# Moving the first FFN's and the branch stage's tiles by 192 bytes in SBUF

## The chip, the cores and the metric

The kernel runs on one core of one Trainium2 chip. The metric is the device time of one execution in microseconds (us). A matmul needs two instructions on TensorE (PE): a weight load, which puts the stationary operand (128 by 128 numbers) into the array, and the matmul itself, which streams the moving operand (here mostly 128 partitions by 512 fp32 numbers) through it into PSUM, the accumulator memory. Both operands lie in SBUF, the on-chip memory of 128 partitions; "the address" of a tile is its byte offset within a partition.

## The reference

One layer on 512 tokens of width 1024, in fp32:

```python
mod = silu(c) @ w_ada + b_ada                  # nine vectors: sh, sc, g for three parts
u = rms_norm(x) * (1 + sc1) + sh1
x = x + 0.5 * g1 * (silu(u @ Wa) * (u @ Wb)) @ ffn1_w_out     # FFN of inner width 2816
u = rms_norm(x) * (1 + sc2) + sh2
z = u @ w_mix + b_mix                          # q, k, v, gates of two branches
y_a = sigmoid(o) * norm(mlstm(q, k, v, i, f))  # 4 heads
y_b = forgetting_attention(q, k, v, f)         # 16 heads of 64
merged = sigmoid(g_a) * (y_a @ w_branch_a) + sigmoid(g_b) * (y_b @ w_branch_b)
x = x + g2 * (merged @ w_out)
u = rms_norm(x) * (1 + sc3) + sh3
x = x + 0.5 * g3 * (silu(u @ Wa2) * (u @ Wb2)) @ ffn2_w_out
```

## The kernel before

**Products in three parts.** Every large product is computed from operands that are split into a high and a low part: `split` (L92 to 105) copies a weight chunk to `wh` on ScalarE (ACT, L102) and subtracts to get `wl` on VectorE (DVE, L104). `mm3` then issues three matmuls, high by high (L127), high by low (L128) and low by high (L129); which operand is the stationary one depends on the stage:

```python
        pin(mm(ps, lh, rh, start=start, stop=False))      # L127: lh stationary, rh moving
        pin(mm(ps, lh, rl, start=False, stop=False))      # L128
        self.last_mm = pin(mm(ps, ll, rh, start=False, stop=stop))   # L129
```

In the profile a group is written out<-moving,stationary with the tiles' names, so `t<-wh,A` streams a weight tile `wh` against the stationary tile `A` and writes PSUM tile `t`.

**Stages and their operands, in order of time.**

- Start (to about 60 us) and the first FFN's input product `ffn_in` (to 268 us): weights `wh`, `wl` stationary, the normed input `uh`, `ul` moving.
- The first FFN's output product `pair_out` (268 to 379 us): stationary are the activations `A1`, `A2` (tags A0 to A10) and their rest tiles `Ra`, `Rb`; moving are the weights `wh`, `wl`. It runs over 11 pairs of row blocks twice: the first pass has 18 matmuls a pair, the second 24, so 462 in all. The second pass adds what the first left to `x` (`onto`, L600) and loads `x` again for that. For the last three pairs a part of the weights is prepared early in tiles `we`, which lie in the same pool as `A`; they are the moving operand of 36 of the matmuls.
- The norm between FFN and mixer, the gates and the attention stage (to about 845 us): two kinds of heads, whose small matmuls and transposes are mixed by hand with the large products of `w_mix`.
- The branch stage (845 to 970 us): `branch` makes 16 products of 24 matmuls, weights stationary, `yh`, `yl` moving; then `token_gemm` multiplies by `w_out` in two halves of 96 matmuls, here `mh`, `ml` stationary and weights moving.
- The second FFN (to the end), the same code as the first: `ffn_in_halves`, `ffn_in`, `pair_out`.

**Order.** Each engine takes its instructions in program order. Loads of weights are issued by SyncE (SP) in program order into a ring of three `raw` tiles; `wh` and `wl` are rings of four. So the chain that feeds PE is: load into `raw`, ACT makes `wh`, DVE makes `wl`; a tile of the rings comes free when PE has used it.

**Where the tiles lie.** Tiles are laid out in pools, one pool behind the other, each tile rounded up to 32 bytes. The pools `w` (weights), `u`, `x` and `y` hold for all or most of the kernel. Behind them pools are opened and closed: `f1t`, `st`, `f1h` for the first FFN, then `y`, and behind it `gates`, `att` (attention) and `br` (branch), then `f2t`, `f2h` for the second FFN. In the program as laid out before the change the tiles that matmuls read start at these addresses modulo 256:

| tiles | pool | address modulo 256 |
|---|---|---|
| weights `raw`, `wh`, `wl`; `uh`, `ul`; `x`; all of the `qk` ring | w, u, x, y | 160 |
| `A1`, `A2`, `Ra`, `Rb`, `we` of the first FFN | f1h, f1t | 224 (rest tiles of pairs 0 to 3: 160, in `x`) |
| `W`, `S`, `P` tiles, `tok` tiles of the attention | att | 0 |
| `vm` ring of the attention | att | 64, 128, 192 |
| `mh`, `ml`, `yh`, `yl`, `sg` of the branch stage | br | 224 |
| `A1`, `A2`, `Ra`, `Rb`, `we` of the second FFN | f2h | 160 |

The 224 comes from two small tiles. In `f1t`, `warm` (4 bytes) and `z22` (16 bytes) take 32 bytes each and stand ahead of everything else but two tiles of 512 bytes: 160 + 64 = 224. In `y`, `hgg` (64 bytes) is the last tile: 160 + 64 = 224 for the pools behind it. All large tiles are multiples of 256 bytes, apart from those of the ring `vm` and three of 32 bytes in `att`.

Of the kernel before, what the change touches and what calls it, by code (L numbers as in the profile page):

```python
# [11 lines left out]
F32 = mybir.dt.float32  # L12
F32R = mybir.dt.float32r
I32 = mybir.dt.int32
AF = mybir.ActivationFunctionType
# [5 lines left out]
P = 128  # L21
# [3 lines left out]
NK = 8  # L25
# [22 lines left out]
class Layer:  # L48
# [109 lines left out]
    def consts(self, tp):  # L158
        nc, cp, A = self.nc, self.cp, self.A
        row = lambda ap: ap.rearrange("o (r p) -> (o r) p", p=P)  # L160
        bm = A["b_mix"]

        self.rowsC = tp.tile([32, P], F32, name="rowsC")
        for r, ap in ((0, row(A["c"])), (8, row(A["ffn1_norm_g"])), (16, row(A["b_ada"][:, 0:2048]))):
            nc.scalar.dma_start(self.rowsC[r:r + ap.shape[0], :], ap)
        self.ident = cp.tile([P, P], F32, name="ident")
        make_identity(nc, self.ident)
        self.one = cp.tile([P, 1], F32, name="one")
        nc.gpsimd.memset(self.one, 1.0)
        self.rowsA = tp.tile([P, P], F32, name="rowsA")  # L170
        put = lambda r, ap: nc.gpsimd.dma_start(self.rowsA[r:r + ap.shape[0], :], ap)
        put(R_N2, row(A["mix_norm_g"]))
        put(R_N3, row(A["ffn2_norm_g"]))
        put(R_CW, A["conv_w"][0].rearrange("j (m p) -> (j m) p", p=P))
        put(R_CB, row(A["conv_b"]))
        put(R_QK, row(bm[:, 0:1024]))
        put(R_GG, row(bm[:, GA:GA + 2048]))
        put(R_MG, A["mlstm_norm_g"][0].rearrange("h (r p) -> (h r) p", p=P))
        put(R_FQ, A["fox_q_norm_g"][0].rearrange("(r h) p -> r (h p)", h=2))
        put(R_FK, A["fox_k_norm_g"][0].rearrange("(r h) p -> r (h p)", h=2))  # L180
        put(R_OM, row(bm[:, OM:OM + 1024]))

        warm = tp.tile([P, 1], F32, name="warm")
        nc.scalar.activation(warm, self.one, AF.Silu)
        z = tp.tile([P, 2, 2], F32, name="z22")
        nc.gpsimd.memset(z, 0.0)
        for h in range(2):
            nc.gpsimd.memset(z[:, h, h:h + 1], 1.0)

        self.unit = cp.tile([P, 2, 2], F32R, name="unit")  # L190
        nc.scalar.activation(self.unit, z, AF.Copy)
        self.mod_d = self.dp.tile([9, D], F32, name="mod_d")
# [1089 lines left out]
    def run(self):  # L1282
        nc, tc, A = self.nc, self.tc, self.A
# [133 lines left out]
        yp = ys.enter_context(tc.tile_pool(name="y", bufs=1))  # L1417
# [18 lines left out]
        with tc.tile_pool(name="att", bufs=1) as ip:  # L1436
            self.maskM = ip.tile([P, P], F32, name="maskM")
            self.maskF = ip.tile([P, P], F32, name="maskF")
            for t, fill, sgn in ((self.maskM, BIG, 1), (self.maskF, -BIG, -1)):

                nc.gpsimd.memset(t, 0.0)
                nc.gpsimd.affine_select(t, t, pattern=[[sgn, P]], compare_op=ALU.is_ge, fill=fill,
                                        base=0, channel_multiplier=-sgn)
            self.onz = ip.tile([P, NT, 2], F32, name="onz")
            nc.gpsimd.memset(self.onz[:, :, 0:1], 1.0)
            nc.gpsimd.memset(self.onz[:, :, 1:2], 0.0)
            self.hom = ip.tile([P, NK], F32, name="hom")
            nc.vector.tensor_scalar(self.hom, self.colA[:, R_OM:R_OM + NK], 0.5, None, op0=MUL)
            self.hmg = ip.tile([P, NK], F32, name="hmg")
            nc.vector.tensor_scalar(self.hmg, self.colA[:, R_MG:R_MG + NK], 0.5, None, op0=MUL)  # L1450
            self.hgg = yp.tile([P, 2 * NK], F32, name="hgg")
            nc.vector.tensor_scalar(self.hgg, self.colA[:, R_GG:R_GG + 2 * NK], 0.5, None, op0=MUL)
            self.klz = [None] * 2
            self.vt, self.W, self.fx, self.qkt, self.S = [None] * 4, {}, {}, {}, {}
            def advance(gen, n):
                for _ in range(n):
                    next(gen, None)
            advance(self.v_mlstm(0, ip, ip), 99)

            gates = iter([(m, i) for i in range(2) for m in range(NK)][2:])  # L1460
            def with_gates(gen, n):
                yield from gen
                for m, i in (next(gates) for _ in range(n)):
                    yield from self.gate(m, i, ip)
            for h0, n, fill in ((0, 3, with_gates(self.v_mlstm(1, ip, ip), 1)), (2, 4, with_gates(self.fox_qkv(0, ip), 3))):
                for f, h in ((self.mlstm_w, h0), (self.mlstm_w, h0 + 1), (self.mlstm_h, h0), (self.mlstm_h, h0 + 1)):
                    f(h, ip)
                    advance(fill, n)
                    if f == self.mlstm_h and h == 2:
                        self.fox_t(0, yp)  # L1470
                advance(fill, 99)
            for n in range(18):
                if n % 4 == 0 and n < 16:
                    advance(fill, 99)
                    g = n // 4
                    fill = with_gates(self.fox_qkv(g + 1, ip), (2, 2, 6)[g]) if g < 3 else (s for m in range(NK) for s in self.y_a(m, yp, ip))
                last = n >= 12
                if n < 16:
                    self.fox_s(n, ip)
                    advance(fill, 4 if n == 0 else 3 if n == 1 else 1 if last else 2)  # L1480
                if n >= 2:
                    self.fox_o(n - 2, ip)
                    advance(fill, 1)
                if n % 2 and n < 13:
                    self.fox_t((n + 1) // 2, yp)
                    if n == 11:
                        self.fox_t(7, yp)
                if 1 <= n < 17:
                    self.fox_p(n - 1, ip)
                    advance(fill, 1 if last else 2)  # L1490
            advance(fill, 99)
            for m in range(NK):
                self.dump(f"ya_{m}", self.ya[m])
                self.dump(f"yb_{m}", self.yb[m])
# [94 lines left out]
```

## Time and profile before

| | |
|---|---|
| median of 3 runs | 1327.01 us (1326.8 to 1328.08) |
| the profiled execution | 1328.68 us, span 1326.9 us from its first to its last instruction |
| PE busy | 1308.3 us, 99% of the span, 6332 matmuls |
| DVE, ACT, POOL busy | 959.9, 622.6, 43.8 us |
| PE's share of the chain that ended last | 91% |
| DMA | 254.18 MB, mean 192 GB/s |

A matmul of 512 columns is shown with a duration of about 0.39 us, though the next one starts after about 0.23 us: they overlap. So the busy time of PE says little, and what counts is the distance from start to start. The duration shown is that distance plus a constant, which is why a group whose matmuls follow one another more slowly by some ns shows a mean that is longer by the same ns.

### The profile page before, as it was taken

The page shows a single profiled execution, that of the slowest core. Times are in us where ns is not written, and L with a number is a line of the kernel's source. Part 1 is how long each engine was busy: PE and PEld are TensorE (multiplying, and loading weights), DVE is VectorE, ACT ScalarE, POOL GpSimd, SP SyncE. Part 2 cuts the span into 40 slices and gives each one's busy share as a digit, 9 for nine tenths or more (in the row PEclk, how much of TensorE's full clock was granted, in tenths as well). Part 3 has the DMA queues.
Part 4 walks back from the last instruction along what each step waited for, and adds up shares of the span by engine and source line. Part 5 has one row for each costly group of instructions (what it writes and reads, how often), then busy time and mean ns, then how long its engine had stood idle before and what let it go on. Part 6 is the DMA issues. An engine that isn't in the chain of part 4 may idle for free.

```text
span 1326.9 us, 17767 instructions
## 1 busy us (share of the span) xinstructions
PE 1308.3 (99%) x6332; PEld 1091.9 (82%) x6332; DVE 959.9 (72%) x1740; ACT 622.6 (47%) x1038; POOL 43.8 (3%) x65
## 2 busy tenths in 40 slices
PE   7999999999999999999999999999999999999998
PEld 6788888888789888888888788888788888888886
DVE  6877777467788687887887778677577656635777
ACT  5533232355476555566566666334263223223742
POOL 1000000000010101000000000003010000000000
PEclk9999999999999999999999999999999999999999
DMA  9899978464845334533342536687429768624574
GB/s 291 265 325 306 315 269 280 127 194 155 291 133 139 110 108 130 159 103 111 91 122 76 170 96 204 214 256 227 155 92 339 264 235 277 210 97 140 170 260 152
DMA packets 204345, 254.18 MB, mean 192 GB/s; under 512 B 14993, under 2 KB 146481, under 8 KB 204257
## 3 DMA queue, kind: packets, MB, share of 16 engines
q1 hardware_dynamic: 203872, 252.98, 59.9%
q8 instruction: 50, 0.82, 0.2%
q14 instruction: 39, 0.31, 0.1%
q0 software_dynamic: 320, 0.06, 0.0%
q10 hardware_dynamic: 64, 0.02, 0.0%
HBM read 217.28 MB, written 35.72 MB: 191 GB/s over the span
## 4 chain that ended last, share of the span: by engine, by line
PE 91%; DVE 4%; ACT 2%; DMA 2%; issue 1%; POOL 0%; SPq 0%; ACTq 0%; DVEq 0%; POOLq 0%
PE g L127 23%; PE g L129 23%; PE g L128 23%; PE t L128 4%; PE t L127 4%; PE t L129 4%; PE g L825 2%; PE t L1208 1%; PE t L1178 1%; DMA x<-x_d 1%; DVE wl L104 1%; PE t L1149 1%; PE t L825 1%; PE t L1150 1%; ACT wh L102 0%
## 5 line engine op out<-in xcount | busy, mean ns | idle before, releaser
L102 ACT ACTIVATE wh<-raw 128x1024 fp32r<-128x1024 f32 (+2 forms) x250 | 253.9, 1018 | 383.0 <-PE g L128 118.4
L104 DVE TENSOR_TENSOR wl<-raw,wh 128x1024 fp32r<-128x1024 f32 (+2 forms) x250 | 292.9, 1174 | 178.0 <-ACT wh L102 154.8
L128 PE MATMUL g<-ul,wh 128*128 128x512 f32 (+1 forms) x912 | 348.1, 383 | 1.0 <-POOL ul L267 1.0
L127 PE MATMUL g<-uh,wh 128*128 128x512 f32 (+1 forms) x912 | 348.5, 384 | 0.0
L129 PE MATMUL g<-uh,wl 128*128 128x512 f32 (+1 forms) x912 | 348.2, 382 | 0.0
L128 PEld LDWEIGHTS g<-ul,wh 128*128 128x128 f32 x912 | 171.3, 188 | 34.3 <-POOL ul L267 1.8
L129 PEld LDWEIGHTS g<-uh,wl 128*128 128x128 f32 x912 | 171.4, 188 | 33.2
L127 PEld LDWEIGHTS g<-uh,wh 128*128 128x128 f32 x912 | 171.0, 188 | 32.8 <-issue 0.6
L325 DVE SCALAR_TENSOR_TENSOR acc<-raw,ccol,acc 128x512 f32<-128x512 f32 (+1 forms) x70 | 66.8, 975 | 43.0 <-DMA raw<-in_w_ada_dram 42.6
L127 PE MATMUL g<-wh,uh 128*128 128x512 f32 (+1 forms) x256 | 97.4, 380 | 0.0
L129 PE MATMUL g<-wh,ul 128*128 128x512 f32 (+1 forms) x256 | 96.6, 377 | 0.0
L128 PE MATMUL g<-wl,uh 128*128 128x512 f32 (+1 forms) x256 | 96.4, 377 | 0.0
L128 PE MATMUL t<-wl,A 128*128 128x512 f32 x176 | 69.3, 394 | 1.7 <-DVE wl L104 1.6
L127 PE MATMUL t<-wh,A 128*128 128x512 f32 x176 | 69.3, 394 | 0.1
L129 PEld LDWEIGHTS g<-wh,ul 128*128 128x128 f32 x256 | 48.2, 188 | 9.0
L127 PEld LDWEIGHTS g<-wh,uh 128*128 128x128 f32 x256 | 48.2, 188 | 8.7 <-DVE tk L1046 0.5
L128 PEld LDWEIGHTS g<-wl,uh 128*128 128x128 f32 x256 | 48.2, 188 | 8.3
L127 PE MATMUL g<-yh,wh 128*128 128x512 f32 x128 | 50.4, 394 | 0.0
L129 PE MATMUL g<-yh,wl 128*128 128x512 f32 x128 | 50.2, 392 | 0.0
L128 PE MATMUL g<-yl,wh 128*128 128x512 f32 x128 | 49.7, 388 | 0.0
L455 ACT ACTIVATE A<-E 128x768 fp32r<-128x768 f32 x22 | 18.6, 846 | 56.5 <-DVE E L454 50.6
L1160 ACT ACTIVATE S<-S,mn 128x128 f32<-128x128 f32 (+1 forms) x64 | 35.5, 556 | 16.1 <-DVE mn L1152 9.9
(343 smaller groups left out, 2187.5 us busy)
## 6 DMA issues: line engine op xcount, KB each, us to landing
raw<-in_ffn_w_in_dram SPq DMA_DIRECT2D x82, 512.0 KB, 5.2
raw<-in_w_ada_dram SPq DMA_DIRECT2D x56, 512.0 KB, 5.1
raw<-in_w_mix_dram SPq DMA_DIRECT2D x46, 512.0 KB, 4.3
sa<-in_ffn_w_out_dram SPq DMA_DIRECT2D x22, 512.0 KB, 5.4
sb<-in_ffn_w_out_dram SPq DMA_DIRECT2D x44, 256.0 KB, 5.9
ws<-sa SPq DMA_DIRECT2D x22, 512.0 KB, 4.5
ws<-sb SPq DMA_DIRECT2D x44, 256.0 KB, 4.1
raw<-ws SPq DMA_DIRECT2D x44, 256.0 KB, 3.4
```

The source lines that it names most:

```text
L102: nc.scalar.activation(hi, src, AF.Copy)
L104: self.last_lo = nc.vector.tensor_tensor(lo, src, hi, op=SUB)
L127: pin(mm(ps, lh, rh, start=start, stop=False))
L128: pin(mm(ps, lh, rl, start=False, stop=False))
L129: self.last_mm = pin(mm(ps, ll, rh, start=False, stop=stop))
L325: nc.vector.scalar_tensor_tensor(a, r[:, s], c, a, op0=MUL, op1=ADD)
L455: nc.scalar.activation(A1[:, 0:3, :], E[:, 0:3, :], AF.Copy)
L825: pin(nc.tensor.matmul(acc_ps[b], (wl if p == 1 else wh)[:, b % 2, s], self.ul[k] if p == 2 else self.uh[k], start=k == 0 and p == 0, stop ...
L1149: nc.tensor.matmul(ps[:, :w], q[:, s], k[:, :w], start=True, stop=False)
L1150: nc.tensor.matmul(ps[:, :w], q[:, s], kl[:, :w], start=False, stop=True)
L1160: nc.scalar.activation(S[:, ws], S[:, ws], AF.Exp, scale=-1.0, bias=m, accum_out=sm[:, qb:qb + 1])
L1178: tr = lambda b, c, qb, kb: nc.tensor.transpose(b[:, c:c + P], S[:, P_OFF[qb] + kb * P:P_OFF[qb] + (kb + 1) * P], self.ident)
```

## The change

Two tiles get more bytes, and what is read and written of them stays the same: `warm` goes from 4 to 224 bytes, `hgg` from 64 to 256. All that lies behind them in SBUF moves up by 192 bytes: in the first FFN the rest of `f1t`, `st` and `f1h`; later `gates`, `att` and `br`. No instruction is added, removed or moved.

```diff
-        warm = tp.tile([P, 1], F32, name="warm")
-        nc.scalar.activation(warm, self.one, AF.Silu)
+        warm = tp.tile([P, 56], F32, name="warm")
+        nc.scalar.activation(warm[:, 0:1], self.one, AF.Silu)
...
-            self.hgg = yp.tile([P, 2 * NK], F32, name="hgg")
+            self.hgg = yp.tile([P, 64], F32, name="hgg")[:, 0:2 * NK]
```

After it, 224 in the table becomes 160 in `f1h`, `f1t` and `br`, 0 becomes 192 in `att`, and the `vm` ring goes to 0, 64, 128. The second FFN's pools do not move, since `f2t` starts where `f1t` and `y` start.

## The prediction

> **What bounds the kernel now.** I began with the page: who is busy, what the clock was, what the last chain consists of.
>
> ```profile
> span 1326.9 us, 17767 instructions
> PE 1308.3 (99%) x6332; PEld 1091.9 (82%) x6332; DVE 959.9 (72%) x1740; ACT 622.6 (47%) x1038; POOL 43.8 (3%) x65
> PEclk9999999999999999999999999999999999999999
> PE 91%; DVE 4%; ACT 2%; DMA 2%; issue 1%; POOL 0%; SPq 0%; ACTq 0%; DVEq 0%; POOLq 0%
> ```
>
> PE sets the end almost everywhere and the granted clock is at 90% or more in every slice, so a change of the time must come from the distance between matmuls or from the few places where PE waits. The change adds no work. The question is only whether that distance depends on where the operands lie. This trace can answer it, because the same code runs twice: the first FFN's output product with its stationary tiles at 224 modulo 256, the second's with them at 160, where the weights are. Next, then, the groups of matmuls with their mean durations, first for the first FFN (268 to 381 us):
>
> ```profile
> L127 PE MATMUL t<-wh,A 128*128 128x512 f32 x88 | 35.0, 398 | 0.1
> ...
> L129 PE MATMUL t<-wh,Ra 128*128 128x512 f32 x20 | 7.9, 396 | 0.0
> ...
> L129 PE MATMUL g<-we,Ra 128*128 128x512 f32 x6 | 2.3, 390 | 0.0
> L129 PE MATMUL g<-we,Rb 128*128 128x512 f32 x6 | 2.3, 389 | 0.0
> ```
>
> and the same view of the second FFN (1215 to 1324 us):
>
> ```profile
> L127 PE MATMUL t<-wh,A 128*128 128x512 f32 x88 | 34.3, 389 | 0.0
> ...
> L127 PE MATMUL g<-wh,A 128*128 128x512 f32 x54 | 20.7, 389 | 0.0
> ...
> L129 PE MATMUL t<-wh,Ra 128*128 128x512 f32 x20 | 7.8, 390 | 0.0
> ```
>
> The reader is to see 396 to 398 ns where moving and stationary operand differ by 64 modulo 256, and 389 to 390 where they agree. The two `we` groups are the control: they run in the first FFN, a few us after the others, with stationary tiles still at 224, but their moving tile lies in the same pool, at 224 too, and they take 389 to 390. So it is not the stage, and not the address itself; it is the difference between the two. The branch stage (845 to 969 us) has both roles reversed:
>
> ```profile
> L129 PE MATMUL g<-yh,wl 128*128 128x512 f32 x113 | 44.3, 392 | 0.0
> L127 PE MATMUL g<-yh,wh 128*128 128x512 f32 x112 | 44.1, 394 | 0.0
> L128 PE MATMUL g<-yl,wh 128*128 128x512 f32 x112 | 43.5, 388 | 0.0
> ...
> L127 PE MATMUL t<-wh,mh 128*128 128x512 f32 x32 | 12.6, 395 | 0.0
> ```
>
> With `yh` moving at 224 and weights at 160 the mean of the three is (392 + 394 + 388) / 3 = 391.3; with `mh` stationary at 224 it is 395.
>
> **The change part by part.** Durations are modelled ends, so I take the distances from starts in the timeline. In the first pass of `pair_out` one pair is 18 matmuls; here is the first matmul of two neighbouring pairs in the first FFN, then the same in the second:
>
> ```profile
> 298.33 0.40 PE L127 MATMUL t<-wh,A 128*128 128x512 f32 x1
> ...
> 302.53 0.40 PE L127 MATMUL t<-wh,A 128*128 128x512 f32 x1
> ```
>
> ```profile
> 1248.20 0.39 PE L127 MATMUL t<-wh,A 128*128 128x512 f32 x1
> ...
> 1252.28 0.39 PE L127 MATMUL t<-wh,A 128*128 128x512 f32 x1
> ```
>
> 4.20 us against 4.08 for 18: 233.3 ns against 226.7, so 6.7 ns a matmul, or 20 ns for each three. The branch product has 24 matmuls a step, and so has a chunk of `w_out`; two neighbouring steps of each:
>
> ```profile
> 878.90 0.39 PE L129 MATMUL g<-yh,wl 128*128 128x512 f32 x1
> ...
> 884.40 0.39 PE L129 MATMUL g<-yh,wl 128*128 128x512 f32 x1
> ```
>
> ```profile
> 923.11 0.39 PE L128 MATMUL t<-wl,mh 128*128 128x512 f32 x1
> ...
> 928.71 0.39 PE L128 MATMUL t<-wl,mh 128*128 128x512 f32 x1
> ```
>
> 5.50 and 5.60 us, where 24 × 226.7 ns is 5.44.
>
> *First FFN's output product.* It counts as far as PE sets the pace. These rows show where it ceases to:
>
> ```profile
> 268.58 0.40 PE L127 MATMUL t<-wh,A 128*128 128x512 f32 x1
> ...
> 354.33 0.40 PE L127 MATMUL t<-wh,A 128*128 128x512 f32 x1
> 354.53 1.06 ACT L102 ACTIVATE wh<-raw 128x1024 fp32r<-128x1024 f32 x1 [2.95 <-PE g L129]
> ...
> 361.56 0.50 PE L127 MATMUL t<-wh,A 128*128 128x512 f32 x1
> 362.82 0.50 PE L128 MATMUL t<-wl,A 128*128 128x512 f32 x1 [0.76 <-DVE wl L104]
> ```
>
> At 361.56 PE stands for 1.26 us for `wl`. The chain behind it goes back to 354.5, where ACT waited 2.95 us for PE to release a `wh` buffer: ACT, DVE, then the next load into `raw`, ACT, DVE. Its length does not change, but its start does, since PE starts it. So all that PE gains up to 354.33 is kept: 354.33 − 268.58 = 85.75 us, 85.75 / 4.20 × 0.12 = 2.45 us. What PE gains from there to 361.56 only makes the wait longer, and behind it the chain runs over the norm on DVE and ACT, so the last 0.4 us or so (some 60 matmuls with `wh` × 6.7 ns) are lost; the `we` matmuls stay at 389. Term: 2.45 us.
>
> *Branch products.* 16 × 24 = 384 matmuls, (391.3 − 389) = 2.3 ns each: 0.9 us. (By the timeline, 16 × 0.06 = 0.96.) No stall of PE in the branch products shows.
>
> *Product with `w_out`.* 8 chunks, 8 × 0.16 = 1.28 us. In its second half the norm of the first 256 tokens is started by the second of four token blocks; this row is PE's transposes for it, which run as soon as DVE delivers:
>
> ```profile
> 964.67 2.14 PE L295 MATMUL t<-ident,xn 128*128 128x128 f32 x16
> ```
>
> The 18 matmuls of the block just before it and the 18 behind it run while DVE and ACT make the norm, so 36 × 6.7 ns = 0.24 are lost. Term: 1.04 us.
>
> *Attention.* Its pool moves too. Inside it every pair of operands keeps its difference. What changes are pairs across pools: a difference of 96 to `u` and `w` becomes 32, one of 128 to `ident` becomes 64. For the transposes the rows say that it does not matter: `ident`, which lies at 128, streams against `xn` at a difference of 96 in the first FFN (first row) and against `S` at 128 in the attention (second row, which holds about 1 us of waits), at the same 272 to 275 ns.
>
> ```profile
> L295 PE MATMUL t<-ident,xn 128*128 128x128 f32 x16 | 1.9, 272 | 0.0
> ```
>
> ```profile
> L1178 PE MATMUL t<-ident,S 128*128 128x128 f32 x160 | 22.1, 275 | 1.0 <-DVE fq L1128 0.5 <-ACT fk L1130 0.3
> ```
>
> No row shows a large matmul at a difference of 32. Such pairs occur where a large product hands over to a head's matmuls, about 36 times. Between the two known ends they cost −6.7 to +6.7 ns each, so ±0.24 us; I take a loss of 0.1, since most differences other than 0 cost something.
>
> Here a rule of the Trainium skill speaks against the change. Its page "TensorE: Matmul & The Clock Gate", section "Part 2: What happens when you issue a matmul", says that PE has two independent read ports into SBUF and that loading the next tile's weights takes no read bandwidth from the running matmul. By that rule no address would matter, every term above would be 0 and the time would stay 1327.0; the rows of `we` (389) beside `wh` (396) in one stage disagree, so the sum goes by the rows.
>
> The sum: 2.45 + 0.9 + 1.04 − 0.1 = 4.3 us. The profiled execution took 1328.68 us (span 1326.9 and 1.8 around it) and would take 1324.4; the median of the runs, 1.67 lower, goes from 1327.01 to 1322.7.
>
> **The rivals.**
>
> *Part of it is given back in new waits.* The second FFN shows what `pair_out` does at the faster pace; it stands twice for `wl`:
>
> ```profile
> 1282.26 0.39 PE L127 MATMUL t<-wh,A 128*128 128x512 f32 x1
> ...
> 1282.78 0.50 PE L128 MATMUL t<-wl,A 128*128 128x512 f32 x1
> ...
> 1293.61 0.39 PE L127 MATMUL t<-wh,A 128*128 128x512 f32 x1
> 1294.79 0.50 PE L128 MATMUL t<-wl,A 128*128 128x512 f32 x1 [0.80 <-DVE wl L104]
> ```
>
> That is 0.52 and 1.18 us where 0.23 is due, 1.24 us together. If the first FFN gets both on top of its own stall, the gain is 4.3 − 1.24 = 3.06 and the time 1324.0; it takes little more (a late weight in the branch stage) to come within 0.2% of no change. For it: the code is the same. Against it: the chain that I followed hangs on PE, and only some 30 matmuls (0.2 us) lie within it.
>
> *The change does nothing.* The difference between the FFNs would have another cause, such as DMA traffic beside them. Then 1327.0; the Trainium skill's page quoted above comes to the same. Against it: `we`, and that both FFNs have the same loads.
>
> *Slower: later landings in the attention's tiles.* These now start 192 past a multiple of 256 rather than on one. Each of the 16 heads needs one broadcast load (`A`) into such a tile before its softmax. The price is bounded by loads of the same 256 KB:
>
> ```profile
> A<-A_d SPq DMA_DIRECT2D x16, 256.0 KB, 4.0
> ...
> sg<-g_d SPq DMA_DIRECT2D x14, 256.0 KB, 2.8
> ...
> ht<-h_d SPq DMA_DIRECT2D x8, 256.0 KB, 2.8
> ```
>
> ```profile
> raw<-ws SPq DMA_DIRECT2D x44, 256.0 KB, 3.4
> ```
>
> `ht` lands on a multiple of 256, `sg` 224 past one, both in 2.8 us: price 0. `raw` from `ws`, 160 past one, takes 3.4: price at most 0.6 a head. All exposed that is 16 × 0.6 = 9.6 us, and 1327.0 − 4.3 + 9.6 = 1332.3. It eats the gain from 0.27 us a head on (4.3 / 16), and makes the kernel slower by over 0.2% from 0.43 on ((4.3 + 2.65) / 16). A rule of the Trainium skill would give such a price: "DMA: Bandwidth & Descriptors", section "How a descriptor splits into AXI transactions", says that a descriptor that doesn't start on 256 bytes needs an extra transaction. `ht` and `sg` don't show it.
>
> **How the numbers follow.** About 0.2% (2.65 us, so below 1324.36 or above 1329.66) is what a measurement of this kernel can tell from no change. The forecast (gain 3.1 to 5.3: all terms with their lost ends given back is 2.85 + 0.96 + 1.28 = 5.1) has 0.70; new waits 0.16, half of it on each side of the bound; nothing 0.08; slower 0.06. Faster: 0.70 + 0.08 = 0.78; same 0.08 + 0.08 = 0.16; slower 0.06. The range goes from the full gain with a little for its chance, 1321.2, to where the new waits are twice as dear, 1325.8; no change and slower are left out.
>
> **What would show it.** In the changed trace, `t<-wh,A` of the first FFN should have a mean near 389 and a pair 4.08 us; `g<-yh,wh` 389 in place of 394, `t<-wh,mh` 389 in place of 395; the wait near 360 us for `wl` should be there still, about 0.2 longer, and start some 2.4 us earlier; from the attention's start to its end the length should be that of before within 0.3 us. The forecast is wrong if these means stay, if the waits for `wl` in the first FFN sum to over 2.5 us, or if the heads wait longer for their `A` tiles.

## The result, and the profile after

| | before | after |
|---|---|---|
| median, beside each other on one chip | 1327.13 us (16 runs, 1325.45 to 1329.57) | 1324.85 us (16 runs, 1323.40 to 1326.66) |
| ratio | 1 | 0.9979, 95% interval 0.9973 to 0.9986 |
| the profiled execution | 1328.68 us, span 1326.9 | 1324.80 us, span 1323.0 |

The kernel became faster by 2.8 us by the ratio (1.9 to 3.6); the medians differ by 2.3. Two later measurements of the same pair, on two chips (7 and 5; `after_again`, `after_third` below), gave 0.9988 (0.9979 to 0.9998) and 0.9987 (0.9978 to 0.9995). The mean of the three ratios is 0.9985: about 2.0 us. The forecast was 4.3 us (1322.7), in a range from 1321.2 to 1325.8. So the direction holds, the time lies in the range, and about half of the forecast gain arrived.

The page of the kernel after: its span, the engines' busy times, and the chain that ended last. PE's share of the chain fell from 91 to 89%, and that of DMA rose from 2 to 3%.

```profile
span 1323.0 us, 17767 instructions
PE 1304.9 (99%) x6332; PEld 1091.7 (83%) x6332; DVE 958.1 (72%) x1740; ACT 624.2 (47%) x1038; POOL 43.7 (3%) x65
...
PE 89%; DVE 4%; DMA 3%; ACT 2%; issue 1%; SPq 0%; POOL 0%; DVEq 0%; ACTq 0%; POOLq 0%
```

The groups of matmuls of the kernel after (busy time, mean ns of one | idle time before them), first in the first FFN's output product, then in the branch stage:

```profile
L127 PE MATMUL t<-wh,A 128*128 128x512 f32 x88 | 34.4, 391 | 0.0
...
L129 PE MATMUL t<-wh,Ra 128*128 128x512 f32 x20 | 7.8, 390 | 0.0
L129 PE MATMUL g<-we,Ra 128*128 128x512 f32 x6 | 2.3, 390 | 0.0
```

```profile
L129 PE MATMUL g<-yh,wl 128*128 128x512 f32 x109 | 42.7, 392 | 0.3 <-DVE wl L104 0.3
L128 PE MATMUL g<-yl,wh 128*128 128x512 f32 x108 | 42.1, 389 | 0.0
L127 PE MATMUL g<-yh,wh 128*128 128x512 f32 x108 | 42.0, 389 | 0.0
...
L127 PE MATMUL t<-wh,mh 128*128 128x512 f32 x32 | 12.5, 389 | 0.0
```

The reader is to see 389 to 391 ns where there were 394 to 398 (`g<-yl,wh`, at 388 before, is at 389), and the control `g<-we,Ra` at its old 390. Two groups are above 389 although their operands now lie at equal addresses: `t<-wh,A` with 391 and `g<-yh,wl` with 392, the latter with 0.3 us of idle time for `wl`. A matmul that had to wait is shown with 500 ns, and that lifts the mean. These are the new waits. The timeline of the kernel after has the pair of the first FFN at the forecast 4.08 us:

```profile
296.87 0.39 PE L127 MATMUL t<-wh,A 128*128 128x512 f32 x1
...
300.95 0.39 PE L127 MATMUL t<-wh,A 128*128 128x512 f32 x1
```

**Where the time went, by stage.** By the names of their tiles, PE executes the same 6332 matmuls in the same order in every kernel below, so a stage's length is the distance between the starts of two given matmuls. These six bound four stages: the first matmul of the first FFN's output product and one of its last, then one in the first and one in the last large product of the attention, then the first of `w_out` and one just behind its end. The timeline of the kernel after:

```profile
267.90 0.39 PE L127 MATMUL t<-wh,A 128*128 128x512 f32 x1
...
375.03 0.39 PE L128 MATMUL g<-we,A 128*128 128x512 f32 x1
...
436.60 0.39 PE L128 MATMUL g<-ul,wh 128*128 128x512 f32 x1
...
826.98 0.39 PE L128 MATMUL g<-ul,wh 128*128 128x512 f32 x1
...
920.16 0.39 PE L128 MATMUL t<-wl,mh 128*128 128x512 f32 x1
...
967.15 0.28 PE L128 MATMUL g<-ul,wh 128*128 128x256 f32 x1
```

and the same six of the kernel before, in a second profile of it that was taken last (`before_again`):

```profile
268.29 0.40 PE L127 MATMUL t<-wh,A 128*128 128x512 f32 x1
...
376.86 0.39 PE L128 MATMUL g<-we,A 128*128 128x512 f32 x1
...
438.52 0.39 PE L128 MATMUL g<-ul,wh 128*128 128x512 f32 x1
...
828.47 0.39 PE L128 MATMUL g<-ul,wh 128*128 128x512 f32 x1
...
923.11 0.40 PE L128 MATMUL t<-wl,mh 128*128 128x512 f32 x1
...
971.10 0.28 PE L128 MATMUL g<-ul,wh 128*128 128x256 f32 x1
```

The same distances for all profiles, in us. The columns "at" give the address modulo 256 of the first FFN's and of the branch stage's tiles; the weights are at 160 in all.

| profile | FFN tiles at | branch tiles at | FFN output | attention | branch | `w_out` |
|---|---|---|---|---|---|---|
| before | 224 | 224 | 109.92 | 389.97 | 92.96 | 47.99 |
| before_again | 224 | 224 | 108.57 | 389.95 | 94.64 | 47.99 |
| warm_only | 160 | 224 | 107.69 | 389.98 | 93.68 | 47.99 |
| hgg_only | 224 | 160 | 108.70 | 390.36 | 94.84 | 46.98 |
| shift_160_224 | 128 | 192 | 109.70 | 390.25 | 94.60 | 47.97 |
| shift_64_32 | 32 | 0 | 109.17 | 390.22 | 94.63 | 48.14 |
| after | 160 | 160 | 107.13 | 390.38 | 93.18 | 46.99 |
| after_again | 160 | 160 | 108.53 | 390.34 | 92.97 | 46.99 |
| after_third | 160 | 160 | 107.48 | 390.36 | 94.16 | 46.98 |
| att160 | 160 | 160 | 109.04 | 389.97 | 92.97 | 46.99 |
| x_late | 160 | 160 | 107.54 | 390.39 | 92.76 | 46.99 |
| yh_first | 160 | 160 | 107.14 | 390.20 | 92.85 | 46.98 |
| three_fixes | 160 | 160 | 108.16 | 389.93 | 92.34 | 46.97 |
| defer | 160 | 160 | 107.34 | 390.28 | 96.76 | 47.00 |

Four things can be read from it. `w_out` gains 1.0 us whenever the branch tiles lie at 160, to within 0.02. The FFN's output product takes 109.2 us on the mean of the five profiles with its tiles elsewhere and 107.8 us on the mean of the nine at 160: 1.4 us, with some overlap (108.57 to 109.92 against 107.13 to 109.04). The attention loses 0.2 to 0.4 us (0.34 in the mean, 0.4 in the three profiles of the changed kernel) in all kernels that move its tiles away from 0, apart from `att160` and `three_fixes`, which move them to 160. And the branch stage gains nothing that can be seen: 93.8 us on the mean of the three profiles with its tiles at 224, 93.6 us on the mean of the five at 160 that change nothing else in it (`hgg_only`, the three of the changed kernel, `att160`). The sum is 1.4 + 0.1 + 1.0 − 0.4 = 2.1 us, which is what the runs give.

### The profile page after: what moved, and what is told of

The parts are those of the page before. It is cut to its first block, busy times and chain, and to the rows that moved or that the text cites. A ratio compares the mean times of both kernels' runs of the same rounds, so it can differ in the third digit from the quotient of the medians.

```text
span 1323.0 us, 17767 instructions
## 1 busy us (share of the span) xinstructions
PE 1304.9 (99%) x6332; PEld 1091.7 (83%) x6332; DVE 958.1 (72%) x1740; ACT 624.2 (47%) x1038; POOL 43.7 (3%) x65
## 4 chain that ended last, share of the span: by engine, by line
PE 89%; DVE 4%; DMA 3%; ACT 2%; issue 1%; SPq 0%; POOL 0%; DVEq 0%; ACTq 0%; POOLq 0%
PE g L129 23%; PE g L127 23%; PE g L128 23%; PE t L128 4%; PE t L129 4%; PE t L127 4%; PE g L825 2%; PE t L1208 1%; PE t L1178 1%; DVE wl L104 1%; DMA x<-x_d 1%; PE t L1149 1%; PE t L825 1%; DMA raw<-in_ffn_w_out_dram 1%; PE t L1150 1%
```

## The experiments

**Each half alone.** My theory was that the distance between matmuls depends on the difference of the two operands' addresses modulo 256. Then each enlarged tile should act in its own stages only.

```diff
 # warm_only: the changed kernel with the second tile as before
-            self.hgg = yp.tile([P, 64], F32, name="hgg")[:, 0:2 * NK]
+            self.hgg = yp.tile([P, 2 * NK], F32, name="hgg")
```

> Only the first FFN's pools move (224 to 160 modulo 256); attention and branch stage stay where they were. The theory that the difference between the two operands' addresses sets the distance of matmuls: in the first FFN a pair of the first pass takes 4.08 us (4.20 before), the stage gains 2.5 to 2.9 us, all of it is still there at the end, and the time is 2.8 us below before. The rival that time gained in one stage is given back at the branch stage's swap of y tiles, because the weights there come by loads that do not start earlier when PE is earlier: the gain is there at 845 us but shrinks by 0.5 to 1 us between 880 and 900 us, and the time is 1.8 to 2.3 us below before.

```diff
 # hgg_only: the changed kernel with the first tile as before
-        warm = tp.tile([P, 56], F32, name="warm")
-        nc.scalar.activation(warm[:, 0:1], self.one, AF.Silu)
+        warm = tp.tile([P, 1], F32, name="warm")
+        nc.scalar.activation(warm, self.one, AF.Silu)
```

> Only gates, attention and branch pools move by 192 bytes; the first FFN keeps its 224. Theory: the branch products gain 0.9 us (g<-yh,wh at 389 in place of 394), the product with w_out 0.8 to 1.0, the attention loses 0.3, and if the swap of y tiles between 880 and 900 us has no room for a faster PE, the 0.9 of the branch is given back there: 0.5 to 0.8 us below before, hard to tell from no change by the time alone. The rival that the swap's loss in the changed kernel was chance of that one execution (a load that landed late): no loss there, 1.4 to 1.7 us below before.

Measured beside a kernel before of 1327.88 us: `warm_only` 1327.08 us, ratio 0.9993 (0.9984 to 1.0001); `hgg_only` 1327.70 us, ratio 0.9999 (0.9990 to 1.0008). In the stages the theory holds: the pace changes only in the FFN's output product in the one and only in branch stage and `w_out` in the other. From start to start, distances over 260 ns left out, the means are 227.1, 229.0 and 233.3 ns in the three stages of `warm_only` and 233.4, 227.1 and 227.3 in `hgg_only`, where the first profile of before has 233.3, 229.0 and 233.3. In the times neither half is to be told from no change: 0.8 and 0.2 us by the medians, less than either theory gave (2.8 or 1.8 to 2.3 for the one, 0.5 to 0.8 or 1.4 to 1.7 for the other). `hgg_only` has its gain in `w_out` (1.0 us) and loses 0.4 in the attention and 1.9 in the branch stage against the first profile of before. What is lost in the branch stage became the question of the later experiments.

**Other addresses.** Is 160 special because it is the weights' address, or is every address better than 224?

```diff
 # shift_64_32: FFN tiles at 32, branch tiles at 0
-        warm = tp.tile([P, 56], F32, name="warm")
+        warm = tp.tile([P, 24], F32, name="warm")
...
-            self.hgg = yp.tile([P, 64], F32, name="hgg")[:, 0:2 * NK]
+            self.hgg = yp.tile([P, 24], F32, name="hgg")[:, 0:2 * NK]
```

> First FFN's tiles move by 64 bytes, to 32 modulo 256, so 128 from the weights; branch stage's by 32 bytes, to 0, so 96 from the weights in the product with w_out. If the period is 256 bytes, only a difference of 0 is free: a pair of the first FFN takes 4.15 to 4.25 us and a step of w_out 5.5 to 5.65, as before. If the period is 128 (or 64), the first FFN comes to 4.08 us a pair at a difference of 128, and w_out stays at 5.6. If instead 160 itself is a good address, both stay as before.

```diff
 # shift_160_224: FFN tiles at 128, branch tiles at 192
-        warm = tp.tile([P, 56], F32, name="warm")
+        warm = tp.tile([P, 48], F32, name="warm")
...
-            self.hgg = yp.tile([P, 64], F32, name="hgg")[:, 0:2 * NK]
+            self.hgg = yp.tile([P, 72], F32, name="hgg")[:, 0:2 * NK]
```

> First FFN's tiles move by 160 bytes, to 128 modulo 256, so 32 below the weights; branch stage's by 224, to 192, so 32 above the weights in w_out. If only an equal address is free, a pair of the first FFN takes 4.15 to 4.25 us and a step of w_out 5.5 to 5.65 us: 32 bytes off is as bad as 64. If the penalty grows with the distance between the addresses, both lie halfway: 4.12 to 4.15 and 5.50 to 5.55 us.

One execution each: 1328.12 and 1329.34 us. Groups of `shift_64_32` and then of `shift_160_224`: FFN, its control with `we`, and branch stage:

```profile
L127 PE MATMUL t<-wh,A 128*128 128x512 f32 x88 | 34.8, 396 | 0.0
...
L129 PE MATMUL g<-we,Rb 128*128 128x512 f32 x6 | 2.3, 389 | 0.0
...
L129 PE MATMUL g<-yh,wl 128*128 128x512 f32 x112 | 44.6, 398 | 0.0
```

```profile
L127 PE MATMUL t<-wh,A 128*128 128x512 f32 x88 | 35.0, 397 | 0.0
...
L129 PE MATMUL g<-we,Rb 128*128 128x512 f32 x6 | 2.3, 391 | 0.0
...
L129 PE MATMUL g<-yh,wl 128*128 128x512 f32 x113 | 44.6, 395 | 0.0
```

An FFN tile 32 bytes below the weights' 160 is as dear as one 64 above (397 against 398 before), and one at 32, which is 128 away, costs 396. So the cost does not repeat every 128 bytes and does not grow with the distance. The branch products are even slower than before: on the mean of all three 233.4 and 233.3 ns from start to start, against 229.0. These rows alone would also fit that 160 is a good address in itself. The control settles it: `we` and its stationary tiles lie at 32 in the one kernel and at 128 in the other, as they lay at 224 before, and their matmuls take 389 to 392. So only the equal address is free, wherever it is.

**The swap of the y tiles.** At about 884 us the branch stage goes over from `ya` to `yb`. `split_y` makes eight new tiles `yh`, `yl` in the buffers that the last product of `ya` is still reading, while the weights of the next products arrive. In the first profile of before PE does not wait there; in the kernel after it waits 0.47 us for `wl` (0.70 us from start to start where 0.23 is due). The timeline of the kernel after:

```profile
876.40 1.06 ACT L102 ACTIVATE wh<-raw 128x1024 fp32r<-128x1024 f32 x1 [1.39 <-DMA raw<-in_w_branch_b_dram]
...
877.36 0.62 ACT L1277 ACTIVATE yh<-yb 128x512 fp32r<-128x512 f32 x1
...
878.01 0.69 DVE L1278 TENSOR_TENSOR yl<-yb,yh 128x512 fp32r<-128x512 f32 x1 [0.78 <-ACT yh L1277]
...
879.95 1.22 DVE L104 TENSOR_TENSOR wl<-raw,wh 128x1024 fp32r<-128x1024 f32 x1
...
880.52 0.39 PE L128 MATMUL g<-yl,wh 128*128 128x512 f32 x1
...
881.22 0.50 PE L129 MATMUL g<-yh,wl 128*128 128x512 f32 x1 [0.32 <-DVE wl L104]
```

and the first profile of before, where PE uses this `wl` at 884.40:

```profile
879.33 1.06 ACT L102 ACTIVATE wh<-raw 128x1024 fp32r<-128x1024 f32 x1 [0.73 <-DMA raw<-in_w_branch_b_dram]
...
880.94 0.69 DVE L1278 TENSOR_TENSOR yl<-yb,yh 128x512 fp32r<-128x512 f32 x1 [0.16 <-ACT yh L1277]
...
882.87 1.22 DVE L104 TENSOR_TENSOR wl<-raw,wh 128x1024 fp32r<-128x1024 f32 x1
```

The chain reads: a weight lands, ACT makes `wh`, only then ACT makes the last `yh`, DVE waits for it (0.78 us in the one, 0.16 in the other) to make the last `yl`, then does two steps for the modulation vector (`acc`), and only then makes `wl`, for which PE waits. Before, `wl` was done at 882.87 + 1.22 = 884.09, 0.31 us ahead of its use. That is thin cover, and the prediction did not reckon with it.

Two theories: (a) the faster products take away the cover; (b) transfers beside it land later. For (b) the loads of `x` were the suspects, since five of eight are issued between 873 and 878 us. Two kernels and, on the same chip, the changed kernel again:

> The changed kernel as it is, once more. If what its first profile showed is its own: FFN pairs at 4.08 us, branch steps at 5.44, w_out steps at 5.44, attention 0.3 us longer than before, and 0.5 to 1 us lost in waits between 880 and 900 us. If the waits there are chance, they are absent or very different. Its time 1.9 to 3.6 us below before, as in the first comparison.

```diff
 # x_late: the changed kernel with the loads of x behind the weights of the fourth yb product
+                if m == 3:
+                    x_after = self.last_raw.ins
...
-            self.x_load(self.x_d)
+            with tc.issue_after(x_after):
+                self.x_load(self.x_d)
```

> The changed kernel, with the eight loads of x for the residual issued after the fourth step of the second branch product, so some 20 us later than now; no other work changes. The theory that their 2 MB make the weights' loads land late at the swap of y tiles: the load issued near 871 us lands in 4.0 to 4.6 us in place of 5.3, the waits between 880 and 900 us go (0.1 us or less in place of 0.9), and the time is 0.9 us below the changed kernel. The rival that the order of work on ACT and DVE makes them late: the load lands as before within 0.5 us, and 0.5 us or more of the waits stay.

```diff
 # defer: the changed kernel with one step of the modulation vectors moved from the swap to the second yb product
-                step()
+                if m < NK - 1:
+                    step()
...
+                if m == 1:
+                    step()
```

> The changed kernel, with one step of the adaLN rows moved from behind the last branch product of the first loop to behind the second of the second loop; ACT then makes the last yh before the next wh, and DVE has two acc operations fewer ahead of that wl. The theory that the order on ACT and DVE makes wl late: wl is done 1.3 us or more earlier against its first use, the waits between 880 and 900 us fall to 0.3 us or less, and the time is 0.6 to 0.9 us below the changed kernel. The rival that the loads' traffic makes it late: 0.5 us or more of the waits stay.

Measured beside a kernel before of 1328.10 us: `after_again` 1326.16 us, 0.9988 (0.9979 to 0.9998); `x_late` 1325.69 us, 0.9985 (0.9977 to 0.9994); `defer` 1329.21 us, 1.0007 (0.9998 to 1.0016). In `x_late`, where the loads of `x` begin at 900 us, the first wait of the swap stays at 0.48 us; the time is the same within the interval. The waits in the next two products (0.18 and 0.11 us in `after`) are gone, but `after_again`, which has the loads of `x` where they were, shows only the second of them. So the loads of `x` are not the cause of the first wait. In `after_again` that wait is 0.17 us, so it varies between executions of one kernel. `defer` does not do what it was meant to: with the step moved, ACT's order came out with the second product's `wh`, behind a wait of 6.03 us for its landing, and work for the modulation vectors ahead of all eight `yh` tiles, which begin at 873.20 us instead of 870.29, and PE then waits for `yl` as well as for `wl` and `wh`. It lost 3.6 us in the branch stage against `after` and says nothing about (a) or (b).

The next kernel cuts the chain itself. It changes the order of one pair of instructions on ACT: the last `yh` ahead of `wh`. The changed kernel ran beside it.

> The changed kernel once more, as the peer of the two kernels beside it on the same chip. Both theories: a ratio to the kernel before of 0.998 to 0.999, a swap of the y tiles (883 to 890 us) that stands 0.4 to 1.0 us longer than two branch steps, and waits for wl in the first FFN that vary by some tenths of a us from execution to execution.

```diff
 # yh_first: the changed kernel; in split, in split_y, and ahead of the yb products
-        with after(self.last_uf):
+        with (self.tc.issue_after(self.yh_last) if getattr(self, "yh_last", None) else after(self.last_uf)):
             nc.scalar.activation(hi, src, AF.Copy)
...
-            nc.scalar.activation(hi, y, AF.Copy)
+            self.yh_ins = nc.scalar.activation(hi, y, AF.Copy).ins
...
+                self.yh_last = self.yh_ins if m == 1 else None
                 t = self.branch(m, 1, bp, None)
```

> One pair of instructions on ACT changes places: the last of the eight yh of branch b is made before wh of the second b product, so that it no longer waits for that weight's landing. If the wait at the swap comes from the chain (landing, wh, then yh, then yl, two acc, then wl on DVE), DVE comes to that wl about 0.8 us earlier, by its 0.78 us of idle time before the last yl; the 0.47 us at the first use of that wl go away, and the 0.1 to 0.3 us in the product behind it with them: 0.5 to 0.9 us less than the changed kernel beside it. If it comes from the landing time of the load itself, the wait stays at 0.4 to 0.7 us and the time is that of the changed kernel.

Beside a kernel before of 1327.77 us: `after_third` 1326.30 us, 0.9987 (0.9978 to 0.9995); `yh_first` 1324.29 us, 0.9978 (0.9969 to 0.9987). The timeline of `yh_first`:

```profile
870.42 5.40 ACT L1277 ACTIVATE yh<-yb 128x512 fp32r<-128x512 f32 x8 [1.97 <-PE g L129]
...
876.21 1.06 ACT L102 ACTIVATE wh<-raw 128x1024 fp32r<-128x1024 f32 x1 [0.40 <-DMA raw<-in_w_branch_b_dram]
...
879.20 1.22 DVE L104 TENSOR_TENSOR wl<-raw,wh 128x1024 fp32r<-128x1024 f32 x1
...
880.87 0.39 PE L129 MATMUL g<-yh,wl 128*128 128x512 f32 x1
...
887.25 0.50 PE L129 MATMUL g<-yh,wl 128*128 128x512 f32 x1 [0.29 <-DVE wl L104]
```

DVE's idle time before the last `yl` is gone, `wl` comes 2.99 us behind the start of `wh` where it was 3.55, and PE uses it with no wait. A wait of 0.46 us remains one product later (887.25), where `after` has 0.18 and the expectation had none; nothing was done about that weight's landing. So the chain is right for the first wait. The medians differ by 2.0 us, more than the 0.5 to 0.9 expected. The two intervals overlap, and the one profile of `yh_first` has a short FFN too (107.14 us); so that the order helps is shown by the trace, by how much is not settled.

Last, the kernel before once more, to see whether the swap waits there too:

> The kernel before once more, for a second look at its stages. If the wait at the swap of the y tiles comes from the faster branch products alone, this profile has none (first use of wl 0.23 us behind its neighbour, 16.96 us from the first to the last product of the swap, as in the first profile). If it comes mostly from a landing that varies from execution to execution, and the first profile of before had a lucky one (4.67 us from issue to wh, against 4.96 to 6.79 in eleven others), this one waits 0.1 to 0.6 us too. In the first FFN both expect 109 to 110 us for the output product, in the attention 389.97 within 0.05, in the second part with w_out 47.99 within 0.05.

1328.40 us, and the answer is clear:

```profile
873.30 0.38 SPq L92 DMA_DIRECT2D raw<-in_w_branch_b_dram  x1
...
879.38 1.06 ACT L102 ACTIVATE wh<-raw 128x1024 fp32r<-128x1024 f32 x1 [2.21 <-DMA raw<-in_w_branch_b_dram]
...
880.99 0.69 DVE L1278 TENSOR_TENSOR yl<-yb,yh 128x512 fp32r<-128x512 f32 x1 [1.58 <-ACT yh L1277]
...
882.74 0.39 PE L128 MATMUL g<-yl,wh 128*128 128x512 f32 x1
...
882.92 1.22 DVE L104 TENSOR_TENSOR wl<-raw,wh 128x1024 fp32r<-128x1024 f32 x1
...
884.19 0.51 PE L129 MATMUL g<-yh,wl 128*128 128x512 f32 x1 [1.06 <-DVE wl L104]
```

This execution of the unchanged kernel waits 1.22 us (884.19 − 882.74 − 0.23), more than the first profile of the changed one and more than the 0.1 to 0.6 expected. Its FFN output product, at 108.57 us, is shorter than the 109 to 110 expected; attention and `w_out` came as expected. From the weight's issue to `wh` it took 879.38 − 873.30 = 6.08 us; the first profile of before has 4.67 us. The other profiles, each read in the same way:

| profile | issue to `wh`, us | wait at the first use of `wl`, us |
|---|---|---|
| before / before_again | 4.67 / 6.08 | 0 / 1.22 |
| warm_only / hgg_only | 5.22 / 6.79 | 0.31 / 1.42 |
| shift_64_32 / shift_160_224 | 5.02 / 5.03 | 0.01 / 0.01 |
| after / after_again / after_third | 5.28 / 4.99 / 5.45 | 0.47 / 0.17 / 1.29 |
| x_late / att160 | 5.28 / 5.31 | 0.48 / 0.50 |
| yh_first / three_fixes (last `yh` first) | 4.96 / 6.14 | 0 / 0.06 |

So theory (a) falls in the form I had given it. From the issue to the moment at which PE wants `wl` there are 9.74 us in the first profile of before and 9.63 in the kernel after: the faster products take away 0.1 us. Most of the rest is the landing, which differs by up to 2 us from execution to execution, over both kernels. The first profile of before had the quickest of all. With the old order on ACT, `wl` is done 4.77 us behind the start of `wh` (3.55 + 1.22), so PE has to wait for what the first column plus 4.77 us exceeds the time from issue to want. That gives each wait in the table that has the old order within 0.06 us. It also gives the one that does not follow from its landing: in `after_third` the load was issued late against PE, with 8.97 us to go, so that 5.45 us cost 1.29, more than the 0.4 to 1.0 expected. With the last `yh` first, a landing of 6.14 us costs 0.06, though that load too was issued late (9.17 us to go).

**The attention.** It lost 0.4 us in the three profiles of the kernel after, which has its tiles at 192. `att160` moves them on to 160 by a larger tile `hmg`, and pads the ring `vm` so that all its buffers lie at 160.

```diff
 # att160: the changed kernel with the attention's tiles at 160
-            t = ap.tile([P, 2, NT, 258], F32R, name=self.nm("vm"), tag="vm", bufs=3)
-            pair = t[:, 0], t[:, 1]
+            t = ap.tile([P, 2, NT, 264], F32R, name=self.nm("vm"), tag="vm", bufs=3)
+            pair = t[:, 0, :, 0:258], t[:, 1, :, 0:258]
...
-            self.hmg = ip.tile([P, NK], F32, name="hmg")
+            self.hmg = ip.tile([P, 48], F32, name="hmg")[:, 0:NK]
```

> The changed kernel, with hmg and the rows of the vm ring enlarged so that the attention's tiles too start at 160 modulo 256 (they were at 0 before the change and at 192 after it). The theory that an unequal address costs wherever a large product hands over to a head's matmuls: from 440 to 840 us the attention takes 0.3 to 0.8 us less than in the changed kernel, so as long as before the change or up to 0.5 us less. The rival that the attention's 0.3 us come from later landings: no change from the changed kernel, within 0.1 us.

One execution, 1324.88 us. The two bounds of its attention:

```profile
438.35 0.39 PE L128 MATMUL g<-ul,wh 128*128 128x512 f32 x1
...
828.32 0.39 PE L128 MATMUL g<-ul,wh 128*128 128x512 f32 x1
```

389.97 us, as before the change, against 390.34 to 390.38 in the three profiles of the kernel after. The loss is gone, though the tiles lie at 160 and not on a multiple of 256. So it is no matter of transfers into tiles that don't start on 256. That the address of the attention's tiles makes the loss is shown; how is not. It does not fit the pairs across pools as I had priced them: at 160 the difference to `u` and `w` is 0, before it was 96, and both give 389.97 us. The loss does not lie in the hand-overs themselves but behind them. Between neighbouring matmuls of the large products (`uh`, `ul` with `wh`, `wl`), whose own operands lie at 160 in every kernel, the distances sum to 278.6 us with the attention's tiles at 0, to 278.9 to 279.1 with them at 192, 224 or 32, and to 278.5 at 160. The number of these 1254 distances that are 230 to 260 ns follows: 253 to 262, 291 to 311, and 239 or 240. All of them are among the first 12 distances of an unbroken row of such matmuls; from the 13th on, each of the 14 profiles has none. So a hand-over leaves the next matmuls slow for a while, and the address of the attention's tiles bears on for how many.

**All three together.**

```diff
 # three_fixes: the edits of yh_first, x_late and att160 in the changed kernel
```

> The changed kernel with yh before wh at the swap, the loads of x behind the weights of the fourth b product, and the attention's tiles at 160 modulo 256. Chain theory: 0.5 to 0.9 us less at the swap and 0.35 us less in the attention, 0.9 to 1.3 us less than the changed kernel in all, so about 1323.5 to 1325 beside a kernel before of 1327 to 1328. If the landing time is what matters at the swap, 0.35 to 0.6 us less.

1324.38 us beside a kernel before of 1327.77, ratio 0.9974 (0.9964 to 0.9983): the best ratio of all, 3.5 us (2.3 to 4.8) below the kernel before. Against the changed kernel beside it the medians differ by 1.9 us; against `yh_first` there is nothing to tell. Its attention (389.93 us) and branch stage (92.34 us) are the shortest in the table. Its interval and that of the changed kernel beside it overlap slightly.

## Why the prediction was half right

*That the distance depends on the difference of the addresses.* Right, at every step: 389 for 394 to 398 ns, 4.08 for 4.20 us a pair, the control unchanged at four addresses, each half acting in its own stages, and no other difference tried that is free. The rival "nothing" falls, and with it what I had drawn from a rule, that no address would matter. The Trainium skill's page "TensorE: Matmul & The Clock Gate", section "Part 2: What happens when you issue a matmul", has loading the next weights take no read bandwidth from the running matmul. In the first FFN the matmuls come every 226.7 ns at equal addresses and every 233.3 ns with the stationary tiles 64 bytes off, with the same instructions. Whether the two reads disturb each other or something else does it, no run here shows.

*Product with `w_out`, 1.04 us.* Right: 1.00 us. The stretch holds nothing that PE waits for but the norm, whose 0.24 I had taken off.

*First FFN's output product, 2.45 us.* The mechanism was right, the size was not: 1.4 us between the means of five and nine profiles. The pace is worth more than I counted (426 matmuls that are not `we` × 6.7 ns = 2.85 us), but about half is given back in waits: summed over the stage, what distances over 0.26 us have beyond 0.23 is 0.3 to 1.7 us in the five profiles (1.0 in the mean) and 1.5 to 3.4 in the nine (2.1). The step that failed is "its length does not change, but its start does, since PE starts it", by which the stall at 361.56 hung on PE and all gain ahead of it was kept. The first two profiles hide it: 109.92 against 107.13 us is a gain of 2.79, but there the distance at the stall went from 1.26 to 1.05 us, where the prediction had it 0.2 longer. That agreement is luck. The second profile of before has no stall there:

```profile
358.75 1.06 ACT L102 ACTIVATE wh<-raw 128x1024 fp32r<-128x1024 f32 x1 [0.82 <-DMA raw<-in_ffn_w_out_dram]
...
359.85 1.22 DVE L104 TENSOR_TENSOR wl<-raw,wh 128x1024 fp32r<-128x1024 f32 x1 [0.66 <-ACT wh L102]
...
361.04 0.40 PE L127 MATMUL t<-wh,A 128*128 128x512 f32 x1
...
361.27 0.40 PE L128 MATMUL t<-wl,A 128*128 128x512 f32 x1
```

and a profile of the kernel after (`after_again`) has it, with the same chain at the same times:

```profile
352.51 1.06 ACT L102 ACTIVATE wh<-raw 128x1024 fp32r<-128x1024 f32 x1 [3.21 <-DMA raw<-ws]
...
358.57 1.06 ACT L102 ACTIVATE wh<-raw 128x1024 fp32r<-128x1024 f32 x1 [1.21 <-DMA raw<-in_ffn_w_out_dram]
...
359.66 1.23 DVE L104 TENSOR_TENSOR wl<-raw,wh 128x1024 fp32r<-128x1024 f32 x1 [1.04 <-ACT wh L102]
...
360.94 0.50 PE L128 MATMUL t<-wl,A 128*128 128x512 f32 x1 [0.76 <-DVE wl L104]
```

`wl` begins at 359.85 in the one and at 359.66 in the other, and ACT waits for landings in both (0.82, 1.21 and 3.21 us). PE started the stage 0.36 us sooner in the second, and its faster pace only brought it to the weight before the weight was there. So these weights hang on the loads at least as much as on PE. At this place two of the five profiles at other addresses show no wait and the other three 0.56 to 1.03 us; all nine at 160 wait, 0.8 to 1.03. The rival "part of it is given back in new waits", to which I gave 0.16, is what happened here: without waits the fast pace would take 108.57 − 2.85 = 105.7 us, and its nine profiles take 107.1 to 109.0. Against it I had argued that the chain I followed hangs on PE; that chain was one execution's. Its sign of being wrong, waits for `wl` of over 2.5 us, does show in two of the nine profiles if all the stage's waits are summed (2.9 in `after_again`, 3.4 in `att160`).

*Branch products, 0.9 us.* "No stall of PE in the branch products shows" was true of the profile and wrong of the kernel. The pace rose about as forecast (229.0 to 227.1 ns, 0.7 us in 384), but the swap waits 0 to 1.4 us by the weight's landing and issue, with the branch tiles at 224 as well as at 160, and the first profile of before was one without. The means over the profiles gain 0.1 us, with a scatter of 1 to 2 us within either group. So whether the pace's gain is there in the time, behind the scatter, stays open. What is shown is that the wait is no product of the change, and that the order on ACT lets a late landing become a wait.

*Attention, −0.1 us.* The sign was right, the size 0.4 us. The step that failed is the place: I priced about 36 matmuls at the hand-overs and let gains and losses cancel, but 0.3 of the 0.4 us lie behind them, between matmuls of the large products, whose operands' addresses did not change. That the sign came out is luck in part.

*Slower by later landings.* It did not come: 0.4 us in 16 heads is 0.02 us a head, where 0.27 would have eaten the gain, and `att160` shows that it is another cause. The loads of `A` take 4.0 us with their tiles at 0, 3.9 at 192 (first profiles) and 4.0 at 160. The rule of the Trainium skill's page "DMA: Bandwidth & Descriptors" (section "How a descriptor splits into AXI transactions") puts extra beats on a descriptor that doesn't start on 256 bytes, and it speaks of what a transaction reads. These loads write the tiles that moved, and no price shows here: tiles at 160 and tiles at 0 both give 389.97 us.

*The sum.* Of the 4.3 us, the FFN lost 1.0, the attention 0.3, the branch products 0.8 (unsettled), which leaves about 2.2 (2.1 by the rounded stage sums above). The measured time lies in the range because the range made room for new waits; its upper end does not follow from its own words, though: twice 1.24 us off 4.3 leaves 1.8, so 1325.2 and not 1325.8. One more thing misled: the first profile of before took 1328.68 us, 1.55 above its median, and part of what it had too much lay in the very stage that I summed (its 109.92 us are the longest of the table), while in the branch stage its 92.96 us are the shortest of all kernels with no edit in that stage but the address.

## What to carry to other kernels

Where fp32 matmuls of 512 columns follow one another with a new weight load each, put moving and stationary tiles at the same address modulo 256: here it cost 192 bytes in each of two tiles and brought up to 7 ns a matmul. Before a faster pace is counted, look for each place where PE's operand is ready by less than the landing of a load varies; a chain with 0.3 us to spare is a wait in the next execution. A single profile gives the pace to a nanosecond, but its waits are a sample of one.

## What was not expected of the hardware

The address effect is sharp. 32 bytes away from the equal address an FFN matmul costs as much as 64 away (397 and 398 ns against 389 to 391), and 128 away hardly less (396). One case is cheaper than the others: with the stationary tile 64 above the moving one all three matmuls of a group take 395 to 398 ns, with the moving tile 64 above the stationary one 388 to 394 (229.0 ns from start to start against 233.3). Whether it is the role or the direction is not shown, since no kernel here has the two apart at 64; at a difference of 32 the moving tile above the stationary one costs 233.3 in the FFN and in the branch products alike. I know no cause for either; the runs show only that equal addresses are free. And even at equal addresses the pace of 227 ns is not always held: in the attention with its tiles at 0, some 250 of the 1254 distances in the large products are 230 to 260 ns, all of them within 12 of a hand-over.

Loads of the same 512 KB weight, from issue to the start of ACT's work on it, took 4.67 to 6.79 us at one place of the program. The loads of `x` were taken away from beside it in two kernels (5.28 and 6.14 us), so they are not the reason. What is stays open.
